# An expert loop with one more block in place of a branch in its middle, and its three compute engines in a written order

## The chip, the cores and the metric

The kernel runs on one core of one Trainium2 chip. The metric is the time of one execution on the device, in microseconds (us). A core has TensorE (PE; its weight loads are shown as PEld), VectorE (DVE), ScalarE (ACT), GpSimd (POOL) and SyncE (SP), each with its own instruction queue; data moves from and to HBM by DMA, which SP, ACT and POOL issue.

## The reference, cut to what matters

A trunk of two layers over 512 tokens of width 1024. Each layer has a mixer, a mixture of experts, and an embedding stage. The change is in the mixture of experts: every token goes to one group of four and in it to the best two of four experts, out of 16.

```python
def hier_moe(x, w_group, b_group, w_router, b_router, w_gate, w_up, w_down):
    ...
    top_v, top_i = lax.top_k(e_sel, TOP_K_IN_GROUP)
    w_k = jax.nn.softmax(top_v, axis=-1) * p_top
    ...
    for e in range(N_EXPERTS):
        he = jax.nn.silu(xt @ w_gate[e]) * (xt @ w_up[e])
        y = y + combine[:, e:e + 1] * (he @ w_down[e])
```

512 tokens with two experts each give 1024 places, 64 for an expert in the mean. A block holds the 128 places of one expert. An expert with more than 128 needs further blocks, which depends on the data; 1024 places fill at most 7 of them.

## The kernel before

All weights stand in one tensor (`wst`) in the order in which they are used: units of 128 x 1024 floats, two of them (1 MB) in a chunk. A block takes 12 units: four for the gate projection, four for the up projection, four for the down projection. `load` (lines 180 to 187) issues one chunk into the next of 14 buffers, which lie in four pools (`RINGS`, line 40); the loads of the loop are issued on SP. `split` (lines 189 to 197) makes from a unit a rounded part `whi` (ACT, line 194) and the remainder `wlo` (DVE, line 195), each with four buffers (`SPLIT`); `mm3` (lines 232 to 235) multiplies with three matmuls, so that the product is nearly that of full floats.

In `moe` (line 925) the router is computed first; it gives the list of places of each expert (`toki`), the list of the further blocks' places (`tokx`, made inside the first block), and `exi` (line 1110), eight integers: for each further block its expert, and in the last the number of further blocks. Then the loop (lines 1238 to 1279) runs over 17 steps: step e gathers the rows of block e+2 (POOL, `gather`), runs gate and up of block e (24 matmuls each), turns the rows of block e+1 (`split_x`: 8 transposes, ACT line 965, DVE line 966), makes the hidden values (`swiglu`, `split_h`: ACT, two DVE operations, 4 transposes, ACT, DVE), and runs the down projection of block e-1 (24 matmuls), whose two halves ACT copies (line 1275) and stores (line 1279, or by halves in line 1277 for the last block). The order on each engine is the scheduler's; the last block's down matmuls run half by half (`DOWN[1]`).

At step `XE` = 5, `further` (line 1187) stands between the hidden values and the down projection: four chunks are loaded ahead, every engine loads the number of further blocks into a register (line 1192), and `blocks` (line 1230) nests seven conditional blocks (`tc.If`, line 1232), each with a whole further block: its weights come by halves of chunks from an address in a register (line 1204), into four single buffers. A conditional block is a unit to the scheduler: nothing from outside moves into it or past it.

After the loop comes `ple` (line 1283), the embedding stage. It loads its first two chunks on SP (lines 1288 and 1289), a third on ACT behind the last store (lines 1291 to 1293), and then runs under a written order for PE, DVE and ACT (`tc.manual_schedule`, line 1295): casts of the first units, 48 matmuls of `project`, the gathers of the expert outputs (line 1312) and so on.

Of the kernel before, what the change touches and what calls it, by code (L numbers as in the profile page):

```python
# [50 lines left out]
XE, XK = 5, 4  # L51

RAWA, RAWB = (2, 3, 1, 0) * 2, (2, 3, 1) * 3
# [53 lines left out]
def tile_hybrid_trunk(ctx, tc, x, wst, gains, small, lam, rwt, cst, out, stop=None):  # L107
# [33 lines left out]
    class W:  # L141
# [8 lines left out]
        base = 0  # L150
# [17 lines left out]
    def pm(shape):  # L168
        return W.psum.tile(shape, F32, name="m", bufs=W.banks["m"])
# [755 lines left out]
    def moe(cx, low, layer):  # L925
# [19 lines left out]
        W.base = FIRST[layer] - PADS[FIRST[layer]]  # L945
# [41 lines left out]
        with ExitStack() as rx:  # L987
# [120 lines left out]
            nc.vector.reduce_sum(exf, xe, axis=AX.X)  # L1108
            nc.vector.tensor_copy(exf[:, 7:8], ext[0:1, 1, NE - 1:NE])
# [57 lines left out]
        with pool_("wk", 2) as wk:  # L1167
# [4 lines left out]
            def swiglu(g, u):  # L1172
                s = wk.tile([128, FF], F32, name="sg", bufs=SB)
                act(s, g, AF.Tanh, scale=0.5)
                stt(s, s, 1.0, g, op0=OP.add, op1=OP.mult)
                tt(s, s, u, op=OP.mult)
                ps = pw([128, 4, 128])
                for f in range(4):
                    nc.tensor.transpose(ps[:, f, :], s[:, f * 128:(f + 1) * 128], ident)  # L1179
                return ps  # L1180

            def split_h(ps, place=None):
                hh, hl = place or [wk.tile([128, 4, 128], F32R, name=n, bufs=HB) for n in ("hh", "hl")]
# [4 lines left out]
            def further(at):  # L1188

                for _ in range(XK):  # L1190
                    ahead()
                nx = nc.values_load(exi[0:1, NX:NX + 1], min_val=0, max_val=NX,
                                    skip_runtime_bounds_check_because="1024 places fill at most 7 further blocks")
                def block(b):
                    ex = nc.sync.value_load(exi[0:1, b:b + 1], min_val=0, max_val=NE - 1)
                    xgx = rows_of(at + 1)
                    nc.gpsimd.indirect_dma_start(out=xgx, out_offset=None, in_=xrow,
                                                 in_offset=bass.IndirectOffsetOnAxis(ap=tokx[:, b:b + 1], axis=0))

                    def part(c, i, a=None):  # L1200
                        n = (RAWA if a else RAWB)[(2 * c + i) % 8]
                        u = wp.tile([128, 1024], F32, name=("wlo", "whi")[n - 2]) if n > 1 else rows_of(at + 1 + n)
                        src = wst[bass.ds(ex * 6 + (FIRST[layer] + c), 1), :, i, :].rearrange("o p b -> (o p) b")
                        nc.sync.dma_start(out=u, in_=src)
                        return split(u, a)

                    split_x(at, xgx)
                    gu = []
                    for m in range(2):
                        ps = pm([128, FF])  # L1210
                        for kp in range(4):
                            w = part(2 * m + kp // 2, kp % 2, 2)
                            for j in range(2):
                                k = 2 * kp + j
                                mm3(ps, xpart(at, k), (w[0][:, j, :], w[1][:, j, :]), k == 0, k == 7)
                        gu.append(ps)
                    hx = rows_of(at + 1, F32R).rearrange("p (h f c) -> p h f c", h=2, f=4)
                    hh, hl = split_h(swiglu(*gu), (hx[:, 0], hx[:, 1]))
                    yp = [pm([128, 512]) for _ in range(2)]
                    for f in range(4):  # L1220
                        w = part(10 + f // 2, f % 2)
                        for nh in range(2):
                            r = slice(nh * 512, (nh + 1) * 512)
                            mm3(yp[nh], (hh[:, f, :], hl[:, f, :]), (w[0][:, r], w[1][:, r]), f == 0, f == 3)
                    y = rows_of(at + 1)
                    for nh in range(2):
                        nc.scalar.copy(y[:, nh * 512:(nh + 1) * 512], yp[nh])
                    nc.scalar.dma_start(out=yrow[(NE + b) * 128:(NE + b + 1) * 128, :], in_=y)

                def blocks(b):  # L1230
                    if b < NX:
                        with tc.If(nx > b):
                            block(b)
                            blocks(b + 1)

                blocks(0)

            hs = None
            for e in range(NE + 1):
                if e < NE:  # L1240
                    if e + 2 < NE:
                        xg.append(gather(toki[:, e + 2:e + 3])[0])
                    gu = []
                    for m in ("gate", "up"):
                        ps = pm([128, FF])
                        for kp in range(4):
                            w = pre.pop(0) if pre else unit(m, 2)
                            for j in range(2):
                                k = 2 * kp + j
                                mm3(ps, xpart(e, k), (w[0][:, j, :], w[1][:, j, :]), k == 0, k == 7)  # L1250
                        gu.append(ps)
                        if m == "gate" and e + 1 < NE:
                            split_x(e + 1, xg[e + 1])
                    if e == 0:

                        wh = wk.tile([128, FF], F32, name="sg", bufs=SB).bitcast(BF)
                        wh = wh.rearrange("p (a t b) -> p a t b", a=2, t=T)
                        nc.vector.tensor_copy(tokx, tokens(slot, wx, NX, wh))
                    with tc.high_priority(offset=40):
                        hh, hl = split_h(swiglu(*gu))  # L1260
                last, hs = hs, (hh, hl)
                if e == XE:
                    further(e)
                if e:
                    yp = [pm([128, 512]) for _ in range(2)]
                    w = {}
                    for f, nh in DOWN[e == NE]:
                        if f not in w:
                            w[f] = unit("down")
                        r = slice(nh * 512, (nh + 1) * 512)  # L1270
                        mm3(yp[nh], (last[0][:, f, :], last[1][:, f, :]), (w[f][0][:, r], w[f][1][:, r]), f == 0, f == 3)
                    y = rows_of(e - 1)
# [254 lines left out]
```

## Time and profile before

| what | value |
|---|---|
| median of three runs | 1467.43 us (1467.11 to 1471.57) |
| the profiled execution's own time | 1475.78 us |
| its span, first to last instruction | 1474.0 us |
| PE busy | 1381.5 us, 94% of the span |
| DVE busy | 1112.3 us, 75% |
| ACT busy | 918.9 us, 62% |
| POOL busy | 127.7 us, 9% |
| mean granted TensorE clock | 0.973 of full speed |

The shares are means over stages that differ. The expert loops run from about 312 to 646 us (layer 0) and from about 1096 to 1400 us (layer 1) of the span. A matmul's duration in the timeline is longer than its step, since matmuls overlap; steps are read from starts. "q" behind an engine's name marks what its sequencer does: issuing DMAs, branches, semaphores, register loads.

### The profile page before, as it was taken

What the parts mean: (1) busy time and instruction counts of PE and PEld (TensorE: products, weight loads), DVE (VectorE), ACT (ScalarE), POOL (GpSimd) and SP (SyncE); (2) the same over time, 40 slices, a digit from 0 to 9 for tenths busy, and PEclk for the clock granted to TensorE, in tenths of its full rate; (3) what the DMA queues carried; (4) which work ended last, traced back from release to release, by engine and by line L of the source; (5) the groups of instructions that cost most, each with busy time, mean ns of one, the idle gap of its engine ahead of it and who ended that gap; (6) DMA issues with size and microseconds to landing.
All of it is one profiled execution on the core that took longest, in us unless ns stands there. A gap on an engine that the chain in (4) does not pass through costs nothing. (4 is left out here: it accounts for less than half of the span.)

```text
span 1474.0 us, 18496 instructions
## 1 busy us (share of the span) xinstructions
PE 1381.5 (94%) x6728; PEld 1091.8 (74%) x6728; DVE 1112.3 (75%) x1573; ACT 918.9 (62%) x1428; POOL 127.7 (9%) x139
## 2 busy tenths in 40 slices
PE   6999999969978999999999999999959979999996
PEld 4766777758856888877878877777648868888775
DVE  5488557689957999977876556665589969999875
ACT  4266654448846888874653545443348858888855
POOL 2010101010000000020020010100010000000030
PEclk9999999979999999999999999999979989999999
DMA  9223124679977999744221111011669979999261
GB/s 343 95 86 129 58 86 172 248 257 381 400 278 290 403 408 408 269 166 192 88 86 57 58 58 57 30 58 61 254 243 346 416 301 390 409 410 386 90 250 58
DMA packets 54650, 323.27 MB, mean 219 GB/s; under 512 B 6480, under 2 KB 6896, under 8 KB 23568
## 3 DMA queue, kind: packets, MB, share of 16 engines
q1 hardware_dynamic: 36576, 250.38, 44.3%
q0 software_dynamic: 12640, 52.16, 9.4%
q10 hardware_dynamic: 5328, 19.40, 3.3%
q8 instruction: 57, 0.93, 0.3%
q14 instruction: 49, 0.40, 0.1%
HBM read 292.55 MB, written 27.26 MB: 217 GB/s over the span
## 5 line engine op out<-in xcount | busy, mean ns | idle before, releaser
L195 DVE TENSOR_TENSOR wlo<-raw,whi 128x1024 fp32r<-128x1024 f32 x478 | 565.0, 1221 | 89.0 <-ACT whi L194 87.0
L194 ACT CAST whi<-raw 128x1024 fp32r<-128x1024 f32 x478 | 492.2, 1055 | 144.4 <-PE m L235 100.7
L233 PE MATMUL m<-whi,eh 128*128 128x512 f32 x528 | 213.9, 405 | 1.6 <-ACT whi L194 1.6
L234 PE MATMUL m<-wlo,eh 128*128 128x512 f32 x528 | 210.9, 399 | 1.6 <-DVE wlo L195 1.5
L235 PE MATMUL m<-whi,el 128*128 128x512 f32 x528 | 210.1, 398 | 0.0
L233 PE MATMUL m<-xth,whi 128*128 128x512 f32 (+1 forms) x368 | 142.9, 389 | 0.6 <-ACT xth L257 0.5
L235 PE MATMUL m<-xth,wlo 128*128 128x512 f32 (+1 forms) x368 | 142.6, 388 | 0.5 <-DVE wlo L195 0.5
L234 PE MATMUL m<-xtl,whi 128*128 128x512 f32 (+1 forms) x368 | 142.0, 386 | 0.8 <-DVE xtl L258 0.8
L234 PEld LDWEIGHTS m<-wlo,eh 128*128 128x128 f32 x528 | 100.5, 190 | 26.6 <-DVE wlo L195 4.2
L233 PE MATMUL m<-whi,xth 128*128 128x512 f32 x288 | 117.0, 406 | 2.7 <-ACT xth L257 1.1
L233 PEld LDWEIGHTS m<-whi,eh 128*128 128x128 f32 x528 | 100.4, 190 | 25.1 <-ACT whi L194 2.1
L235 PEld LDWEIGHTS m<-whi,el 128*128 128x128 f32 x528 | 100.0, 189 | 24.4 <-DVE el L966 0.8
L235 PE MATMUL m<-whi,xtl 128*128 128x512 f32 x288 | 115.7, 403 | 1.6 <-DVE xtl L195 1.0
L234 PE MATMUL m<-wlo,xth 128*128 128x512 f32 x288 | 115.4, 401 | 0.5 <-DVE wlo L195 0.5
L233 PE MATMUL m<-whi,hh 128*128 128x512 f32 x256 | 103.6, 410 | 0.0
L235 PE MATMUL m<-whi,hl 128*128 128x512 f32 x256 | 102.4, 400 | 0.0
L234 PE MATMUL m<-wlo,hh 128*128 128x512 f32 x256 | 102.1, 400 | 0.0
L235 PEld LDWEIGHTS m<-xth,wlo 128*128 128x128 f32 x368 | 70.5, 192 | 12.8 <-DVE wlo L195 1.0
L234 PEld LDWEIGHTS m<-xtl,whi 128*128 128x128 f32 x368 | 70.4, 191 | 12.6 <-DVE xtl L258 1.0
L233 PEld LDWEIGHTS m<-xth,whi 128*128 128x128 f32 x368 | 70.5, 192 | 12.5 <-ACT xth L257 0.9
L973 POOL DMA_INDIRECT xg<-xrow,toki x32 | 34.5, 1079 | 494.8 <-PE w L963 439.2
L965 ACT CAST eh<-w 128x512 fp32r<-128x512 f32 x82 | 46.9, 590 | 39.4 <-PE w L963 38.1
(445 smaller groups left out, 2268.3 us busy)
## 6 DMA issues: line engine op xcount, KB each, us to landing
raw<-in_wst_dram SPq DMA_DIRECT2D x226, 1024.0 KB, 7.5
raw<-in_wst_dram POOLq DMA_DIRECT2D x14, 1024.0 KB, 7.5
yrow<-y ACTq DMA_DIRECT2D x17, 512.0 KB, 8.4
yrow<-gbc ACTq DMA_DIRECT2D x14, 512.0 KB, 8.0
xrow<-raw POOLq DMA_DIRECT2D x8, 512.0 KB, 5.7
yrow<-tmp POOLq DMA_DIRECT2D x14, 256.0 KB, 10.0
h<-in_x_dram SPq DMA_DIRECT2D x4, 512.0 KB, 13.4
whi<-in_wst_dram SPq DMA_DIRECT2D x4, 512.0 KB, 5.4
```

The source lines that it names most:

```text
L194: nc.scalar.copy(hi, src)
L195: nc.vector.tensor_sub(lo, src, hi.bitcast(F32))
L233: mm(ps, l[0], r[0], start=start, stop=False)
L234: mm(ps, l[0], r[1], start=False, stop=False)
L235: mm(ps, l[1], r[0], start=False, stop=stop)
L965: W.turned = nc.scalar.copy(eh[o], ps)
L973: ins = nc.gpsimd.indirect_dma_start(out=xg, out_offset=None, in_=xrow, in_offset=bass.IndirectOffsetOnAxis(ap=idx, axis=0))
```

## The change

The first further block becomes a block of the loop, always run, after expert 5 (`BLOCKS`); where the data needs none, it runs on places that nobody reads (its expert is limited to 15 by a minimum on `exf`). Its six chunks are loaded like the others, from an address in a register of SP. Blocks 2 to 7 stand in nested conditional blocks behind the loop, the outermost with the skipped arm preferred to follow in the code; inside (`rare`) all is single-buffered, and the store is issued by POOL. The register with the number of further blocks is loaded ahead of the loop. From block 1 on the loop stands under a written order for PE, DVE and ACT, in which the casts of a block's units are spread over its own step and the one before.

```diff
-XE, XK = 5, 4
-RAWA, RAWB = (2, 3, 1, 0) * 2, (2, 3, 1) * 3
+BLOCKS = [0, 1, 2, 3, 4, 5, NE] + list(range(6, NE))
+RAWA = (0, 1, 2, 0, 1, 2, 0, 1)
...
-            ring = W.rings[RINGS[(c - W.base - PADS[c]) % len(RINGS)]]
+            ring = W.rings[RINGS[W.count % len(RINGS)]]
+            W.count += 1
...
             nc.vector.reduce_sum(exf, xe, axis=AX.X)
+            ts(exf, exf, NE - 1.0, None, op0=OP.min)
...
-            def further(at):
-                for _ in range(XK):
-                    ahead()
-                nx = nc.values_load(exi[0:1, NX:NX + 1], min_val=0, max_val=NX,
...
-            hs = None
-            for e in range(NE + 1):
...
-                if e == XE:
-                    further(e)
...
+            def rare(at, b):
+                ex = nc.sync.value_load(exi[0:1, b:b + 1], min_val=0, max_val=NE - 1)
...
+                nc.gpsimd.dma_start(out=yrow[(NE + b) * 128:(NE + b + 1) * 128, :], in_=y)
+                if b + 1 < NX:
+                    with tc.If(nx > b + 1, preferred_fallthrough_block=True):
+                        rare(at, b + 1)
+            CHUNK = {"g": 0, "u": 2, "d": 10}
+            extra, parts = {}, {}
+            def chunk(e, m, k):
+                i = CHUNK[m] + k // 2
+                if e == NE:
+                    if i not in extra:
+                        if not extra:
+                            W.ex = nc.sync.value_load(exi[0:1, 0:1], min_val=0, max_val=NE - 1)
+                        src = wst[bass.ds(W.ex * 6 + (FIRST[layer] + i), 1)].rearrange("o p u b -> (o p) u b")
+                        extra[i] = load(src)
+                    return extra[i]
+                c = FIRST[layer] + 6 * e + i
+                if c not in W.loaded:
+                    W.loaded[c] = load(wst[c])
+                return W.loaded[c]
+            def high(e, *units):
+                for m, k in units if e is not None else ():
+                    src = chunk(e, m, k)[:, k % 2, :]
+                    w = [wp.tile([128, 1024], F32R, name=n) for n in ("whi", "wlo")]
+                    nc.scalar.copy(w[0], src)
+                    parts[e, m, k] = src, *w
+            def low_(e, *units):
+                for m, k in units if e is not None else ():
+                    src, hi, lo = parts[e, m, k]
+                    nc.vector.tensor_sub(lo, src, hi.bitcast(F32))
...
+            G, U = [[(m, k) for k in range(4)] for m in "gu"]
+            nx = nc.values_load(exi[0:1, NX:NX + 1], min_val=0, max_val=NX,
...
+            order = ExitStack()
+            order.enter_context(tc.manual_schedule(engines=MS))
+            both(BLOCKS[1], *G, *U[:3])
+            for j, e in list(enumerate(BLOCKS))[1:]:
+                last = BLOCKS[j - 1]
+                q = BLOCKS[j + 1] if j + 1 < len(BLOCKS) else None
+                if j + 2 < len(BLOCKS):
+                    xg.append(rows(BLOCKS[j + 2]))
+                g = pm([128, FF])
+                for k in range(4):
+                    towards(g, j, "g", e, k)
+                turned = [turn_x(j + 1, xg[j + 1], half) for half in range(2)] if q is not None else []
+                s = wk.tile([128, FF], F32, name="sg", bufs=SB)
+                for i in range(3):
+                    if i == 1:
+                        act(s, g, AF.Tanh, scale=0.5)
+                        stt(s, s, 1.0, g, op0=OP.add, op1=OP.mult)
+                    elif turned:
+                        ps, o = turned.pop(0)
+                        nc.scalar.copy(eh[o], ps)
+                        nc.vector.tensor_sub(el[o], ps, eh[o].bitcast(F32))
+                both(e, U[3])
+                both(last, ("d", 0), ("d", 1))
+                u = pm([128, FF])
+                for k in range(4):
+                    towards(u, j, "u", e, k)
+                tt(s, s, u, op=OP.mult)
+                both(last, ("d", 2), ("d", 3))
+                high(q, G[0])
+                yp = [pm([128, 512]) for _ in range(2)]
+                for f in range(2):
+                    down(yp, hs, last, f)
+                now = split_h(turned_s(s))
+                for f in range(2, 4):
+                    down(yp, hs, last, f)
+                low_(q, G[0])
+                both(q, *G[1:3])
+                y = rows_of(j)
+                for nh in range(2):
+                    nc.scalar.copy(y[:, nh * 512:(nh + 1) * 512], yp[nh])
+                store(last, y)
+                hs = now
+                both(q, G[3], *U[:3])
+            e = BLOCKS[-1]
+            both(e, *[("d", f) for f in range(4)])
+            yp = [pm([128, 512]) for _ in range(2)]
+            y = rows_of(len(BLOCKS))
+            for nh in range(2):
+                r = slice(nh * 512, (nh + 1) * 512)
+                for f in range(4):
+                    down(yp, hs, e, f, nh)
+                nc.scalar.copy(y[:, r], yp[nh])
+                put = store(e, y, r)
+            order.close()
+            W.pos = [i for i, u in enumerate(UNITS) if u == ("pp", 0)][layer]
+            W.next = W.pos // 2
+            with tc.If(nx > 1, preferred_fallthrough_block=False):
+                rare(len(BLOCKS) + 1, 1)
```

`both` is `high` (the cast on ACT) followed by `low_` (the remainder on DVE), unit by unit; `towards` gives the six matmuls of one gate or up unit, `down` the matmuls of one down unit, `turn_x` the transposes of the next block's rows, `turned_s` those of the hidden values, `store` the store on ACT.

## Rows read from the trace of the kernel before

**Rows 1.** Busy time by stretch, two stretches of layer 0's expert loop: its undisturbed part, and one period of it. Columns: stretch, its length, busy us (x instructions) of PE, PEld, DVE, ACT and POOL, granted TensorE clock, DMA share, GB/s.
```profile
480.00:640.00 160.00, 160.00 (x742) 130.25 (x741) 151.62 (x150) 134.22 (x158) 5.68 (x6) 1.00 0.85 340
500.00:518.09 18.09, 18.09 (x86) 14.75 (x85) 17.12 (x18) 15.24 (x19) 0.95 (x1) 1.00 1.00 409
```

**Rows 2.** The timeline of PE at the end of layer 0's loop and the start of the next stage. Columns: start us, us, engine, line, operation, output and inputs, tile, count, and in brackets the idle time before it with its releaser. The first row is the first of the last block's down matmuls, the second the last of them (23 steps further); the third is the third matmul of the next stage; the fourth the first transposes of that stage.
```profile
639.99 0.39 PE L233 MATMUL m<-whi,hh 128*128 128x512 f32 x1
645.35 0.39 PE L235 MATMUL m<-whi,hl 128*128 128x512 f32 x1
...
647.02 0.50 PE L235 MATMUL m<-whi,xtl 128*128 128x512 f32 x1 [0.53 <-DVE xtl L195]
...
658.94 1.29 PE L255 MATMUL w<-cs,h 128*128 128x128 f32 x8 [0.92 <-DVE h L1317]
```

**Rows 3.** The timeline of ACT in both loops, the issues of a block's output store alone, on either side of the branch (layer 0: between the second and third row; layer 1: between the sixth and seventh). Columns as in rows 2.
```profile
383.34 0.33 ACTq L1279 DMA_DIRECT2D yrow<-y  x1
401.42 0.33 ACTq L1279 DMA_DIRECT2D yrow<-gbc  x1
...
461.59 0.33 ACTq L1279 DMA_DIRECT2D yrow<-y  x1
478.92 0.33 ACTq L1279 DMA_DIRECT2D yrow<-gbc  x1
...
1167.74 0.33 ACTq L1279 DMA_DIRECT2D yrow<-y  x1
1185.83 0.33 ACTq L1279 DMA_DIRECT2D yrow<-gbc  x1
1215.57 0.34 ACTq L1279 DMA_DIRECT2D yrow<-y  x1
1232.89 0.33 ACTq L1279 DMA_DIRECT2D yrow<-gbc  x1
```

**Rows 4.** The timeline of ACT in the undisturbed period, around the copies of a block's output.
```profile
514.00 1.07 ACT L1275 COPY gbc<-m 128x512 f32<-128x512 f32 x2
514.96 1.07 ACT L194 CAST whi<-raw 128x1024 fp32r<-128x1024 f32 x1
515.10 0.33 ACTq L1279 DMA_DIRECT2D yrow<-gbc  x1
```

**Rows 5.** The timeline of ACT at the end of layer 0's loop. L194 casts one unit of weights, L1275 copies half an output, L1279 and L1277 are stores, L1286 is the next stage's table load.
```profile
638.79 1.05 ACT L194 CAST whi<-raw 128x1024 fp32r<-128x1024 f32 x1 [0.34 <-PE m L235]
639.75 1.07 ACT L1275 COPY y<-m 128x512 f32<-128x512 f32 x2
640.70 1.06 ACT L194 CAST whi<-raw 128x1024 fp32r<-128x1024 f32 x1
643.22 1.05 ACT L194 CAST whi<-raw 128x1024 fp32r<-128x1024 f32 x1 [1.46 <-PE m L235]
...
644.65 1.05 ACT L194 CAST xth<-raw 128x1024 fp32r<-128x1024 f32 x1
...
646.39 0.33 ACTq L1277 DMA_DIRECT2D yrow<-gbc  x1
646.75 1.28 ACT L1286 ACT_TABLE_LOAD   x1 [0.39 <-ACT gbc L1275]
```

**Rows 6.** The timeline of DVE in the undisturbed period: three remainders of weight units in a row.
```profile
512.18 3.48 DVE L195 TENSOR_TENSOR wlo<-raw,whi 128x1024 fp32r<-128x1024 f32 x3
```

**Rows 7.** The branch's own instructions, by engine and operation: those of DVE in layer 1 (two rows), and those of PE's sequencer in layer 0 (three branches, of which the first lets the entered arm follow). Columns: line, engine, operation, count: duration in ns (min/median/max), first and last start in us.
```profile
L1232 DVEq COMPARE_BRANCH  x1: 69/69/69, 1199.7 to 1199.7; - x1
L1232 DVEq EVENT_SEMAPHORE  x1: 21/21/21, 1205.5 to 1205.5; - x1
...
L1232 PEldq COMPARE_BRANCH  x3: 86/192/3848, 414.2 to 451.5; - x3
```

**Rows 8.** Layer 0's branch as SP sees it: SP's semaphore instructions of the branch (columns as in rows 7); the further block's store and its time from issue to landing; SP's first issue of weights after the branch (columns as in rows 2).
```profile
L1232 SPq EVENT_SEMAPHORE  x9: 17/17/17, 444.4 to 452.6; - x9
...
L1228 ACTq DMA_DIRECT2D yrow<-y x1: 331/331/331, 449.7 to 449.7; - x1
...
DMA to landing us min/median/max: 2.9/2.9/2.9
...
452.95 0.35 SPq L186 DMA_DIRECT2D raw<-in_wst_dram  x1
```

**Rows 9.** SP's last issues of weights in layer 0 before the next stage (columns as in rows 7), and three lines of the DMA issues of the whole span: out and in, queue, operation, count, KB each, median us from issue to landing. The third is the store of half the last block's output, the fourth the load that ACT issues behind it.
```profile
L186 SPq DMA_DIRECT2D raw<-in_wst_dram x3: 328/328/328, 602.1 to 607.7; - x3
...
raw<-in_wst_dram SPq DMA_DIRECT2D x226, 1024.0 KB, 7.5
...
yrow<-gbc ACTq DMA_DIRECT2D x4, 256.0 KB, 2.1
...
raw<-in_wst_dram ACTq DMA_DIRECT2D x2, 1024.0 KB, 5.2
```

**Rows 10.** Busy time by stretch behind layer 0's branch; columns as in rows 1.
```profile
452.00:454.00 2.00, 2.00 (x9) 1.97 (x10) 1.46 (x2) 2.00 (x3) 0.00 (x0) 0.50 0.26 41
456.00:458.00 2.00, 2.00 (x8) 1.59 (x8) 1.64 (x3) 1.05 (x1) 0.00 (x0) 0.78 1.04 365
```

**Rows 11.** The register loads of the expert list in both layers, on DVE and on PE's sequencer; columns as in rows 7.
```profile
L1192 PEldq TENSOR_LOAD <-exi x2: 318/402/486, 413.6 to 1198.0; - x2
...
L1192 DVEq TENSOR_LOAD <-exi x2: 316/430/543, 414.9 to 1199.3; - x2
```

More of the change, by code (lines that the diff above doesn't have):

```diff
@@ L1186, in split_h @@
                 return hh, hl
-            def further(at):
-                for _ in range(XK):
-                    ahead()
-                nx = nc.values_load(exi[0:1, NX:NX + 1], min_val=0, max_val=NX,
[L1193 to L1236, printed above, removed]
@@ L1238, in moe @@
-            hs = None
-            for e in range(NE + 1):
[L1240 to L1261, printed above, removed]
-                if e == XE:
-                    further(e)
[L1264 to L1272, printed above, removed]
@@ new lines, in rare, with part @@
+            def rare(at, b):
+                ex = nc.sync.value_load(exi[0:1, b:b + 1], min_val=0, max_val=NE - 1)
+                xgx = rows_of(at)
+                nc.gpsimd.indirect_dma_start(out=xgx, out_offset=None, in_=xrow,
+                                             in_offset=bass.IndirectOffsetOnAxis(ap=tokx[:, b:b + 1], axis=0))
+                def part(c, i, a=None):
+                    n = RAWA[2 * c + i] if a else i
+                    u = wp.tile([128, 1024], F32, name=("wlo", "whi")[n]) if n < 2 else rows_of(at)
+                    src = wst[bass.ds(ex * 6 + (FIRST[layer] + c), 1), :, i, :].rearrange("o p b -> (o p) b")
+                    nc.sync.dma_start(out=u, in_=src)
+                    return split(u, a)
+                split_x(at, xgx)
+                gu = []
+                for m in range(2):
+                    ps = pw([128, FF])
+                    for kp in range(4):
+                        w = part(2 * m + kp // 2, kp % 2, 2)
+                        for j in range(2):
+                            k = 2 * kp + j
+                            mm3(ps, xpart(at, k), (w[0][:, j, :], w[1][:, j, :]), k == 0, k == 7)
+                    gu.append(ps)
+                s = product(*gu, rows_of(at)[:, :FF])
+                hx = rows_of(at, F32R).rearrange("p (h f c) -> p h f c", h=2, f=4)
+                hh, hl = split_h(turned_s(s), (hx[:, 0], hx[:, 1]))
+                yp = [pw([128, 512]) for _ in range(2)]
+                for f in range(4):
+                    w = part(10 + f // 2, f % 2)
@@ new lines, in both, with towards, down @@
+            def both(e, *units):
+                for u in units if e is not None else ():
+                    high(e, u)
+                    low_(e, u)
+            def towards(ps, j, m, e, k):
+                _, *w = parts[e, m, k]
+                w = [a.rearrange("p (a b) -> p a b", a=2) for a in w]
+                for i in range(2):
+                    mm3(ps, xpart(j, 2 * k + i), (w[0][:, i, :], w[1][:, i, :]), k == i == 0, 2 * k + i == 7)
+            def down(yp, h_, e, f, *halves):
+                _, *w = parts[e, "d", f]
+                for nh in halves or range(2):
+                    r = slice(nh * 512, (nh + 1) * 512)
+                    mm3(yp[nh], (h_[0][:, f, :], h_[1][:, f, :]), (w[0][:, r], w[1][:, r]), f == 0, f == 3)
@@ new lines, in turn_x, with store, rows @@
+            def turn_x(j, src, half):
+                ps = pw([128, 4, 128])
+                for d in range(4):
+                    k = 4 * half + d
+                    nc.tensor.transpose(ps[:, d, :], src[:, k * 128:(k + 1) * 128], ident)
+                return ps, (slice(None), j % 2, slice(4 * half, 4 * half + 4))
+            def store(e, y, r=slice(None)):
+                return nc.scalar.dma_start(out=yrow[e * 128:(e + 1) * 128, r], in_=y[:, r])
+            def rows(e):
+                return gather(tokx[:, 0:1] if e == NE else toki[:, e:e + 1])[0]
@@ new lines, in moe @@
+            G, U = [[(m, k) for k in range(4)] for m in "gu"]
+            nx = nc.values_load(exi[0:1, NX:NX + 1], min_val=0, max_val=NX,
+                                skip_runtime_bounds_check_because="1024 places fill at most 7 further blocks")
+            xg.append(rows(BLOCKS[2]))
+            gu = []
+            for m in ("gate", "up"):
+                ps = pm([128, FF])
+                for kp in range(4):
+                    w = pre.pop(0) if pre else unit(m, 2)
+                    for j in range(2):
+                        k = 2 * kp + j
+                        mm3(ps, xpart(0, k), (w[0][:, j, :], w[1][:, j, :]), k == 0, k == 7)
+                gu.append(ps)
+                if m == "gate":
+                    split_x(1, xg[1])
```

31 lines of the change are left out of this document (21 added, 10 removed).

## The prediction

> **What bounds the kernel now.** I read first the busy time by stretch, because the change touches only the expert loop of each layer. In the undisturbed stretch of layer 0's loop PE is busy 160.00 of 160 us, and in one period of it 18.09 of 18.09, with DVE at 17.12 and ACT at 15.24 [rows 1]. The reader should see that TensorE alone sets the pace, that DVE has only 0.97 us to spare in a period, and that a full period costs 18.09 us whatever the queues do. The arithmetic agrees: 72 matmuls in steps of 0.233 us (23 steps from 639.99 to 645.35 [rows 2]) are 16.8, and 12 transposes take what is left.
>
> Next come the issues of the output stores, one for each block, as a clock of the loop [rows 3]. Between branches they stand 18.09 apart. Across layer 0's branch, which runs one further block, the next two distances are 60.17 and 17.33, so 77.50 in place of 36.18: **this branch costs 41.3 us**. Across layer 1's branch, which runs none, they are 29.74 and 17.32: 47.06 in place of 36.18, so **a branch that is not entered costs 10.9 us**. (The 17.3 is the part that is given back, so both are counted over two distances.) One of the two layers needs one further block, the other needs none, and no layer needs a second.
>
> Then the branch's own instructions and the seam behind the loop, since that is where the branch goes.
>
> **The change part by part.** The sum is made against the profiled execution, 1475.8 us (span 1474.0 and 1.8 around it). That is 8.3 above the median of the runs, 1467.43, so differences are added to the median. About 0.3% of it, 4.4 us, is what a measurement can tell from no change.
>
> *The blocks.* Layer 0 loses the 41.3 and gains one period: 18.1 - 41.3 = **-23.2**. Layer 1 loses 10.9 and gains a period that computes nothing of use: 18.1 - 10.9 = **+7.2**. The extra block's six loads, its gather and its store go at the rate of the others (409 GB/s in the period [rows 1], so 7.4 MB) behind PE. Its loads take their address from a register of SP, which costs SP instructions that the 14 loads in flight cover; if the cover is gone it is under a microsecond. [...]
>
> *The fixed order.* In the period the scheduler of before put on ACT three casts, three more, the cast of the hidden values, two casts, two copies and then the next casts. The change writes out the same order, with one difference: the store is issued before the next cast, not behind it. Now the cast starts at 514.96, before the copies end at 515.07, and the store follows at 515.10 [rows 4]. The cast would start at about 515.45, 0.5 us later, and the unit it makes is wanted by PE only 3 us after (18 matmuls into the next block). DVE's 0.97 us of spare time takes it up. I take 0; a gain is excluded because PE is already full, and if the cover fails the price is at most the 0.34 of an issue for each of 32 periods, 11 us.
>
> *The last block.* Here the fixed order matters. Now ACT casts the last block's down weights ahead of and between the copies (638.79, 640.70), so the 24 last matmuls run without a gap, 24 x 0.233 = 5.6 us [rows 2, 5]. In the change all four casts are written behind the two copies and the store of the block before. Count from A, the start of the last down matmuls: copies end at A+0.83, the store is issued until A+1.2, the first cast ends at A+2.25, and four subtractions in steps of 1.16 [rows 6] end at A+7.0. PE can then finish half one (to A+7.4) and run the 12 matmuls of half two (2.8): it ends at A+10.2. That is **+4.6** a layer, 9.2 in all. Waiting behind the copies are DVE's subtractions and through them PE; nothing else fills PE there.
>
> *The branch at the end.* What a branch does is in layer 1's rows [rows 7]: the compare itself takes 0.05 to 0.07 us, but DVE goes on only 5.8 us later (1199.7 to 1205.5), and everything waits for DVE. In the change the skipped arm is the one that follows in the code. In layer 0, where the entered arm follows, PE's shortest compare is 0.09 us. I take 0.1 (nearest row), with 5.8 as the upper end. [...]
>
> What is not free is what stands behind it. [...] Layer 0 shows it: the further block's store was issued at 449.7, landed 2.9 us later, and only then (last of nine, 452.6) did SP pass and issue its next weights at 452.95 [rows 8]. In the change the last store of the loop stands in front of the branch, and the next stage's weights behind it. Now SP issues those some 38 us earlier, at 602.1 to 607.7, against a last store at 646.39 [rows 5, 9]. Let B be the end of the last down matmuls, 645.6 now. The last store is issued at B+0.8, lands 2.1 us later [rows 9], SP issues at B+3.3, 1 MB lands 5.2 us later (the two that ACT issues at this place [rows 9]) at B+8.5. ACT casts two units by B+10.5, DVE has the second remainder at B+11.7, and only then can the third matmul of the next stage run. Now that is at 647.02, B+1.4 [rows 2]. So **+10.3** a layer, 20.6 in all. The ends: 4.3 if SP is not held (then only the table load of 1.28, two casts and a subtraction are in the way, third matmul at B+5.7), 12.6 if the load takes 7.5 like SP's others [rows 9].
>
> *The clock.* After the idle stretch before 451.9 the granted clock was 0.50 and came back at about 456.5 [rows 10]; half of 4.6 us is lost. The same after the new gap: **+2.3** a layer, 4.6 in all. None is lost in the gap of 2.3 us at A, I take it; if it is, 2 more.
>
> *The rest.* The register loads from the expert list move ahead of the loop, 0.3 to 0.54 us each [rows 11], on engines that work there: 0.5 a layer, 1.0. The one added minimum on eight numbers is nothing. Back comes the 0.92 in which PE waits for the gathered rows in the next stage [rows 2], since the stores are late by less (4.6) than PE (14.9): -1.3 over both layers.
>
> Sum: -23.2 + 7.2 + 9.2 + 20.6 + 4.6 + 1.0 - 1.3 = **+18.1**, so 1485.5 us (chance 0.5). Its own range is 1476 to 1496.
>
> **The rivals.** *SP is not held.* If the stores' semaphores are none of those SP brings up, the weights are there and each seam costs 4.3, not 10.3: 18.1 - 12.0 = +6.1, 1473.5. For it: the rare arm's own store has moved from ACT to POOL. Against: its twelve loads a block still use SP's semaphores, and [rows 8] show SP wait for an ACT store. Chance 0.18.
>
> *Faster: the seam is covered.* The blocks save 16.0 us; the edges of the two loops decide, and the point is 8.0 us a layer. If the next stage's weights and casts are as early as now, only the last block's 4.6 and the 0.5 are left: -16.0 + 9.2 + 1.0 = -5.8, 1461.6; with the last casts in time as well, 1452. For it: PE has 24 matmuls in hand while ACT and SP pass the branch. Against: every instruction of the next stage is behind the branch on its engine, and ACT's last copy stands in front. Chance 0.2.
>
> *The fixed order costs in every period.* DVE is at 95%, so the later cast may reach PE: +11 on the forecast, 1496.5. For it: the small slack. Against: the wait is 3 us from its user. A skip that still jumps belongs here too; with SP held its 5.8 lie beside the load. Chance 0.12.
>
> **How the numbers follow.** The likeliest is 1485.5. Faster is most of the second rival, 0.18; within 0.3% is half of the first and a little of the second, 0.12; the rest, 0.70, is slower. The range leaves out the covered seam at its best and the worst of the last rival: 1461 to 1502.
>
> **What would show it.** In the changed profile: stores 18.09 apart through all 17 blocks of both layers, with no gap at the former branch; a gap of PE of 2.3 us before the last down matmuls, and these lasting about 10; SP's next weights issued some 3 us after the last store; PE idle about 10 us there and the clock at 0.50 after it. Wrong would be: weights of the next stage issued long before the last store (first or second rival), or stores more than 18.2 apart (third).

## The result, and the profile after

The kernel with the change takes 1478.79 us (median of 12 runs, 1476.89 to 1483.05), the kernel before beside it on the same chip 1471.64 (12 runs, 1465.41 to 1476.76): ratio **1.0055**, interval 1.0039 to 1.0071, so slower by 8.1 us by this ratio (5.7 to 10.4; the two medians are 7.2 apart). The prediction had the sign and its range held the time, but its sum, +18.1, was more than twice too large. The profiled execution took 1478.86 (span 1476.8).

First the busy time by stretch of the changed kernel: one period of layer 0's loop, as in the second row of [rows 1], and stretches behind the places where PE idles, as in [rows 10].

```profile
500.00:518.09 18.09, 18.09 (x85) 14.74 (x85) 16.96 (x18) 15.03 (x19) 0.95 (x1) 1.00 1.00 398
...
620.00:622.00 2.00, 2.00 (x7) 1.48 (x6) 2.00 (x3) 0.74 (x1) 0.00 (x0) 0.50 0.00 0
...
634.00:636.00 2.00, 2.00 (x7) 1.57 (x6) 0.74 (x1) 1.23 (x2) 1.69 (x3) 0.56 0.86 233
...
1388.00:1392.00 4.00, 4.00 (x11) 3.12 (x10) 2.73 (x3) 0.91 (x1) 0.00 (x0) 0.50 0.01 2
```

The period is untouched: PE fills all of it, DVE has 1.13 us to spare. The stores, read as in [rows 3] from ACT's timeline (some of both layers, the last full period among them), say the same of the whole loop:

```profile
418.41 0.33 ACTq L1297 DMA_DIRECT2D yrow<-gbc  x1
436.50 0.33 ACTq L1297 DMA_DIRECT2D yrow<-y  x1
...
599.27 0.33 ACTq L1297 DMA_DIRECT2D yrow<-gbc  x1
...
1132.32 0.33 ACTq L1297 DMA_DIRECT2D yrow<-y  x1
...
1367.44 0.33 ACTq L1297 DMA_DIRECT2D yrow<-gbc  x1
```

They stand 18.09 apart (599.27 is nine periods behind 436.50, 1367.44 thirteen behind 1132.32); nothing is left of the branches that cost 41.3 and 10.9 us in [rows 3]. What the change costs is at the loop's end. PE's timeline there, to be read beside [rows 2]: the end of the block before, the gaps in the last block's downs, the last down, and the next stage's first matmul and first transposes (L257), in layer 0, then the same of layer 1.

```profile
615.38 0.40 PE L237 MATMUL m<-whi,hl 128*128 128x512 f32 x1
617.95 0.50 PE L235 MATMUL m<-whi,hh 128*128 128x512 f32 x1 [2.17 <-ACT whi L1262]
619.21 0.79 PE L236 MATMUL m<-wlo,hh 128*128 128x512 f32 x1 [0.76 <-DVE wlo L1269]
...
625.75 0.39 PE L237 MATMUL m<-whi,hl 128*128 128x512 f32 x1
630.33 0.80 PE L235 MATMUL m<-whi,xth 128*128 128x512 f32 x1 [4.19 <-ACT xth L196]
...
644.30 1.03 PE L257 MATMUL w<-cs,h 128*128 128x128 f32 x8
...
1386.12 0.50 PE L235 MATMUL m<-whi,hh 128*128 128x512 f32 x1 [2.17 <-ACT whi L1262]
...
1395.40 0.40 PE L237 MATMUL m<-whi,hl 128*128 128x512 f32 x1
1400.70 0.80 PE L235 MATMUL m<-whi,xth 128*128 128x512 f32 x1 [4.90 <-ACT xth L196]
...
1415.43 1.03 PE L257 MATMUL w<-cs,h 128*128 128x128 f32 x8
```

Two places cost time: the last block's downs, which last from 615.6 to 626.0, and the seam behind the branch, where PE idles 4.19 and 4.90 us, not the 10 predicted. ACT's timeline of the same stretch (as [rows 5]; L1364 copies the block before, whose store comes first; L1262 casts the last down weights, L1376 copies the last block's halves, L196 and L1389 are the next stage's casts and table load, L188 a load for it):

```profile
616.43 0.33 ACTq L1297 DMA_DIRECT2D yrow<-y  x1
616.85 3.88 ACT L1262 CAST whi<-raw 128x1024 fp32r<-128x1024 f32 x4 [0.45 <-ACT y L1364]
...
624.00 0.33 ACTq L1297 DMA_DIRECT2D yrow<-gbc  x1
626.18 0.59 ACT L1376 COPY gbc<-m 128x512 f32<-128x512 f32 x1 [2.21 <-PE m L237]
626.66 1.05 ACT L196 CAST whi<-raw 128x1024 fp32r<-128x1024 f32 x1
...
627.19 1.99 ACTq L188 DMA_DIRECT2D raw<-in_wst_dram  x1
627.73 1.28 ACT L1389 ACT_TABLE_LOAD   x1
629.23 1.04 ACT L196 CAST xth<-raw 128x1024 fp32r<-128x1024 f32 x1 [0.22 <-issue]
```

Last the branch of layer 0 (L1381) by engine, with columns as in [rows 7], to be read beside [rows 7, 8]:

```profile
L1381 SPq COMPARE_BRANCH  x2: 38/46/53, 593.3 to 626.4; - x2
...
L1381 PEldq COMPARE_BRANCH  x2: 98/2016/3935, 623.3 to 626.3; - x2
L1381 ACTq COMPARE_BRANCH  x2: 38/44/49, 624.9 to 625.1; - x2
```

And SP's loads for the next stage (L188), in the same columns, where [rows 9] had SP's last issues at 602.1 to 607.7:

```profile
L188 SPq DMA_DIRECT2D raw<-in_wst_dram x2: 327/328/328, 590.3 to 592.6; - x2
```

Three things are to be seen. SP is indeed held at the branch, from 593.3 to 626.4, that is until 2.4 us behind the issue of the store of 624.00 (such a store lands in 2.1 [rows 9]). But the next stage's first two chunks were issued **ahead** of it, at 590.3 and 592.6, and ACT's last copy, and with it the last store, stands **behind** its branch (625.1, then 626.18): here the scheduler moved independent instructions past the conditional block, in both directions. And each engine has two branch instructions: the compare that falls through (98 ns on PE) and then a second one, which I read as a jump over the code that lies in between, the six rare blocks (e9 tests this reading). It takes PE 3.94 us, to 630.3, just when ACT's cast is done too (629.23 and 1.04).

### The profile page after: what moved, and what is told of

Its sections match the earlier page's. It is cut to its first block, busy times and chain, and to the rows that moved or that the text cites. A ratio compares the mean times of both kernels' runs of the same rounds, so it can differ in the third digit from the quotient of the medians.

```text
span 1476.8 us, 18718 instructions
## 1 busy us (share of the span) xinstructions
PE 1392.1 (94%) x6812; PEld 1104.7 (75%) x6812; DVE 1123.4 (76%) x1592; ACT 928.6 (63%) x1446; POOL 132.4 (9%) x140
## 5 line engine op out<-in xcount | busy, mean ns | idle before, releaser
L1269 DVE TENSOR_TENSOR wlo<-raw,whi 128x1024 fp32r<-128x1024 f32 x392 | 456.6, 1219 | 13.8 <-ACT whi L1262 13.7
L1262 ACT CAST whi<-raw 128x1024 fp32r<-128x1024 f32 x392 | 396.0, 1055 | 50.5 <-PE m L237 36.7
L235 PE MATMUL m<-whi,eh 128*128 128x512 f32 x544 | 218.8, 402 | 0.0
L236 PE MATMUL m<-wlo,eh 128*128 128x512 f32 x544 | 215.5, 396 | 0.0
L237 PE MATMUL m<-whi,el 128*128 128x512 f32 x544 | 215.4, 396 | 0.0
L197 DVE TENSOR_TENSOR wlo<-raw,whi 128x1024 fp32r<-128x1024 f32 x110 | 133.3, 1225 | 69.8 <-ACT whi L196 69.5
L196 ACT CAST whi<-raw 128x1024 fp32r<-128x1024 f32 x110 | 113.9, 1050 | 64.6 <-PE m L237 33.3
L235 PE MATMUL m<-whi,hh 128*128 128x512 f32 x272 | 112.1, 412 | 4.3 <-ACT whi L1262 4.3
L236 PE MATMUL m<-wlo,hh 128*128 128x512 f32 x272 | 109.3, 402 | 1.5 <-DVE wlo L1269 1.5
L237 PE MATMUL m<-whi,hl 128*128 128x512 f32 x272 | 108.8, 400 | 0.0
```

Of the source, the lines that this page charges most:

```text
L196: nc.scalar.copy(hi, src)
L197: nc.vector.tensor_sub(lo, src, hi.bitcast(F32))
L235: mm(ps, l[0], r[0], start=start, stop=False)
L236: mm(ps, l[0], r[1], start=False, stop=False)
L237: mm(ps, l[1], r[0], start=False, stop=stop)
L1262: nc.scalar.copy(w[0], src)
```

## The experiments

The theory that the profile of the change suggested (A): two costs of similar size, the last downs behind late casts (some 4 to 5 us a layer) and the seam behind the branch (4 to 5 us), nothing in the loop, and branches of before that cost less at the median than in the one execution that was profiled. The rivals were that one of the two holds all of it, and that a branch's price does not vary. Ratios are to the kernel before on the same chip; 0.001 is 1.47 us. By the ratios' intervals a difference between two kernels below is uncertain by 3 to 5 us.

**e1: no branch behind the loop.** The register loads and further blocks 2 to 7 are left out (this input needs none).

```
-            nx = nc.values_load(exi[0:1, NX:NX + 1], ...)
...
-            with tc.If(nx > 1, preferred_fallthrough_block=False):
-                rare(len(BLOCKS) + 1, 1)
```

> The changed kernel without the conditional block behind the loop and without the register loads for it (this data never enters it). Theory A, the seam is the branch: PE idles 4.2 and 4.9 us behind the last down matmuls because its second branch instruction takes 3.9 and 3.3 us and because the next stage's two casts may not stand ahead of the branch on ACT. Without it the gap falls to about 0.5 and the clock stays up: 4 + 2 us in each layer, 12 less than the changed kernel's 1478.8, so about 1467. Theory B, the gap is ACT's order (copy, cast, table load, cast) and not the branch: it stays near 4, about 1478.

1471.66 us, ratio 1.0008 (0.9988 to 1.0028): 0.0047 or 6.9 us below the change, where 12 were expected. PE's timeline at both seams (last down, next stage's first matmul, its first transposes; layer 0, then layer 1 without the matmul):

```profile
625.93 0.39 PE L237 MATMUL m<-whi,hl 128*128 128x512 f32 x1
626.68 0.50 PE L235 MATMUL m<-whi,xth 128*128 128x512 f32 x1 [0.36 <-ACT xth L196]
...
639.28 1.29 PE L257 MATMUL w<-cs,h 128*128 128x128 f32 x8 [0.17 <-DVE h L1415]
...
1394.31 0.40 PE L237 MATMUL m<-whi,hl 128*128 128x512 f32 x1
...
1407.35 1.16 PE L257 MATMUL w<-cs,h 128*128 128x128 f32 x8
```

The gap is gone, so it is the branch's. At the seams it is worth what the theory said: from the last down to the first transposes PE takes 13.35 and 13.04 us, in the change 18.55 and 20.03, so 5.2 + 7.0 = 12.2 with the clock's part. But layer 0's share did not last in this execution. PE's first transposes in layer 1's loop wait for gathered rows; in the change:

```profile
1079.70 1.94 PE L965 MATMUL w<-cs,xg 128*128 128x128 f32 x8 [5.79 <-DMA xg<-xrow,toki]
```

And in e1:

```profile
1079.48 1.94 PE L965 MATMUL w<-cs,xg 128*128 128x128 f32 x8 [10.14 <-DMA xg<-xrow,toki]
```

They start at the same time in both. In all other profiles here this wait is 5.6 to 6.6 us; whether other executions of e1 wait so long, and for what, is open.

**e2: the last block's casts first.** The last down weights are cast where another block would cast its next one's gate weights, ahead of and around the copies. Nothing is left out.

```
-                high(q, G[0])
+                z, D = (q, G) if q is not None else (e, [("d", f) for f in range(4)])
+                high(z, D[0])
...
-            both(e, *[("d", f) for f in range(4)])
```

> The changed kernel with the last block's four down casts and remainders in the places that a next block's first four gate units would have, ahead of and right behind the two copies. Theory A, these 4.6 us a layer (and the clock that falls in their gap, 1 to 2 us) are lost to the written order: the last down matmuls run in 5.6 us and not in 10.4 and 11.9, about 10 to 13 less than 1478.8, so 1466 to 1469, with the gap behind the branch unchanged at 4 to 5. Theory B, the time is only moved: PE ends earlier but waits longer behind the branch, 1476 to 1479.

1470.85 us, ratio 1.0000 (0.9984 to 1.0017): 0.0055 or 8.1 us below the change, 4.0 a layer. Two stores of layer 0 (ACT's timeline), of the block before and of the last block's first half, show where:

```profile
616.28 0.33 ACTq L1297 DMA_DIRECT2D yrow<-y  x1
620.38 0.33 ACTq L1297 DMA_DIRECT2D yrow<-gbc  x1
```

The first half's store comes 4.10 behind the block before, not 7.57 (616.43 to 624.00).

**e3: both.** e1 and e2 in one kernel, further blocks 2 to 7 left out.

> Both edits together, no branch and the last casts first. Theory A: the two losses are apart and add, so the blocks' own saving of 16 us against the kernel before stands alone: about 1471.6 - 15 = 1457. Theory B, one loss hides the other: no better than the better of the two, 1466.

1462.72 us, ratio 0.9942 (0.9925 to 0.9960): 16.6 us below the change, where 6.9 and 8.1 make 15.0. The two costs add up; neither hides the other, and without both the change would be faster than before by 0.6%. At the seams e3 takes 13.37 and 13.03 us from the last down to the first transposes, e2 18.35 and 19.42: 11.4 less, of which the time keeps 8.5. So here too part of the gain is lost later: at layer 0's seam e3 gains 5.0 us on e2, of which 1.8 is left when layer 1's first gathered rows come.

**e4: the next stage's weights issued late.** This puts in what the prediction had assumed, that the two chunks are issued behind the last store (here by ACT, in the prediction by SP).

```
-        for i in range(2):
-            ahead(pool=PLACE(i))
+        with tc.issue_after(put.ins):
+            for i in range(2):
+                ahead(nc.scalar, PLACE(i))
```

> The changed kernel with the next stage's first two chunks issued by ACT behind the last store, as the prediction had them, and not some 33 us earlier by SP. Theory A (the prediction's price was right for weights that come late): 1 MB lands 5 to 7 us after its issue at about B+1.6, two casts and a remainder follow, the third matmul of the next stage runs at about B+11 and not at B+5.7: 5 us in each layer and some clock, 1489 to 1492. Theory B, what bounds the seam is PE's branch and ACT's table load, and the loads lie beside them: under 3 us in each layer, 1479 to 1484.

1489.68 us (6 runs), ratio 1.0126 (1.0098 to 1.0154), 10.4 us above the change. PE's timeline, layer 0 and layer 1:

```profile
636.76 0.79 PE L235 MATMUL m<-whi,xth 128*128 128x512 f32 x1 [9.25 <-ACT xth L196]
...
1412.40 0.79 PE L235 MATMUL m<-whi,xth 128*128 128x512 f32 x1 [10.47 <-ACT xth L196]
```

What ACT's cast waits for, from its timeline in layer 0:

```profile
634.72 1.04 ACT L196 CAST whi<-raw 128x1024 fp32r<-128x1024 f32 x1 [4.90 <-DMA raw<-in_wst_dram]
```

The third matmul of the next stage comes 10.7 and 11.9 us behind the last down (638.21 and 1413.85), where the prediction had 11.7. Its price for late weights was right; in the change they are not late.

**e5: the kernel before without its branches.** Layer 0's further block, a part of the result, is left out.

```
-                if e == XE:
-                    further(e)
```

> The kernel before without its branch, its further blocks and their register loads (layer 0's further block is left out). It measures what the change removes. By the store distances of the profiled execution the two branches cost 41.3 + 10.9 = 52.2 us: 1471.7 - 52.2 = 1419.5. Rival: the profiled execution of the kernel before is some 4 us above its median because its branches take longer under the profiler than otherwise (all of its executions spread over 12 us, those of the kernels without a branch over 8); then the saving is 46 to 49, 1423 to 1426.

1419.67 us (5 runs), ratio 0.9679 (0.9658 to 0.9701): the two branches together cost 47.1 us (43.9 to 50.3), not the 52.2 of the profiled execution. (The time is theory A's 1419.5 only because the kernel before took 1467.13 beside it, not 1471.7.)

**e6: the change without its extra blocks.** Layer 0's further block is left out.

```
-BLOCKS = [0, 1, 2, 3, 4, 5, NE] + list(range(6, NE))
+BLOCKS = list(range(NE))
```

> The changed kernel without the extra block (layer 0's further block is left out), the written order and the branch behind the loop kept. It measures what the extra block costs. Theory A: one period in each layer, 2 x 18.09 = 36.2 less than 1478.8, 1442.6. Against e5, which has neither block nor branch, what is left over is the price of the order and of the two seams: 17 to 23 us by the sum's terms as the changed trace shows them. Rival: the extra block also costs DMA time or a wait, 38 or more.

1440.79 us (5 runs), ratio 0.9819 (0.9799 to 0.9838): 0.0236 or 34.7 us below the change, so an extra block costs 17.4, within the error of its 18.09. Against e5, the same blocks with the old loop end, it is slower by 0.0140, **20.6 us: all that the two loop ends cost**, since in both the stores inside the loop stand 18.09 apart.

**e7: the order left to the scheduler.** The hand-written order of the loop is taken out.

```
-            order.enter_context(tc.manual_schedule(engines=MS))
...
-            order.close()
```

> The changed kernel with the loop's written order taken away, so that the scheduler sets the order of PE, DVE and ACT; blocks and branch as in the change. Theory A: the written order gains nothing in the loop (18.09 us from store to store in both) and loses about 4.5 us a layer at the last block, so 8 to 10 less, 1469 to 1471. Theory B: it is needed because the scheduler, given the code in this form, feeds PE worse: over 1479.

1472.06 us, ratio 1.0021 (1.0004 to 1.0038): 5 us below the change. The stores stay 18.09 apart, so the order is worth nothing inside the loop, and costs at its end, where the scheduler casts the last weights earlier. PE's gaps at the seams stay, 6.40 and 4.53.

**e8: the kernel before, once more**, to see whether a branch's price varies.

> The kernel before once more with a profile. Theory A, the first profiled execution was typical: span within 2 us of 1474, 41.3 and 10.9 us at the two branches. Theory B, the branches vary from execution to execution: these two differ by 2 us or more from the first profile.

1468.57 us (one execution). ACT's stores around layer 1's branch, as in [rows 3]:

```profile
1182.36 0.33 ACTq L1279 DMA_DIRECT2D yrow<-gbc  x1
...
1208.71 0.34 ACTq L1279 DMA_DIRECT2D yrow<-y  x1
1226.02 0.33 ACTq L1279 DMA_DIRECT2D yrow<-gbc  x1
```

And what ended PE's idle time in it, from PE's timeline, with DVE's instructions of this branch (columns as in [rows 7]):

```profile
1199.29 1.94 PE L963 MATMUL w<-cs,xg 128*128 128x128 f32 x8 [4.13 <-DVEq L1232]
...
L1232 DVEq COMPARE_BRANCH  x1: 69/69/69, 1196.2 to 1196.2; - x1
...
L1232 DVEq EVENT_SEMAPHORE  x1: 21/21/21, 1199.2 to 1199.2; - x1
```

The same matmul in the first profile of the kernel before:

```profile
1205.59 1.94 PE L963 MATMUL w<-cs,xg 128*128 128x128 f32 x8 [6.95 <-DVEq L1232]
```

The two distances are 26.35 and 17.31, so this branch cost 7.5 us, not 10.9. The price varies from one execution to the next, with the same code and the same data (the first profile's chip is not on record; on one chip the executions of this kernel spread over 13 us). What varied is on DVE: from its compare to its next instruction it took 3.0 us here and 5.8 in [rows 7]. Layer 0's distances are 59.27 and 17.30 here, so its branch cost 40.4. Together that is 47.9, near e5's 47.1, in an execution near the median. So being profiled does not by itself make the branches dear, as e5's rival had it.

**e9 to e11: what the gap at the seam is made of.** All three build on e2, where PE idles 3.98 and 5.31 us. e9 cuts the code behind the branch to one rare block (3 to 7 are left out), so that PE's jump is short (the first edit below); e10 moves the next stage's table load behind the cast of its input (the second); e11 does both.

```
-                if b + 1 < NX:
+                if b + 1 < 2:
...
-        tc.keep_in_program_order(nc.scalar.preload_act_table_set("natural_log_exp_and_others"))
...
         pe_ = unit("p", None, ...)
+        tc.keep_in_program_order(nc.scalar.preload_act_table_set("natural_log_exp_and_others"))
```

> This is the last block with its casts first, with the code behind the branch cut to one rare block (its rare blocks 3 to 7 are left out), so that TensorE's jump over it is short. In the kernel with casts first TensorE's own jump ends at 626.1 us and ScalarE's cast of the next stage's input at 626.4, in the second layer at 1390.5 and 1392.3: two chains that end nearly together. Theory A (both chains are needed): TensorE's second branch falls from 3.4 and 3.3 us to under 0.5, but its gap stays at 3.6 to 4.0 us in the first layer and 4.5 to 5.3 in the second, since ScalarE's chain (copy, cast, store, issue, table load, cast) is as long; the time stays at that of casts first, about 1471 us, within 2 us. Rival B (the far jump alone holds the engines, ScalarE's too): the gap falls to 1 to 2 us in both layers and the time by 5 to 7 us, to 1464 to 1466 us.

> This is the last block with its casts first, with the next stage's table load moved behind ScalarE's cast of that stage's input (nothing left out). ScalarE's chain behind the branch gets shorter by the table load's 1.28 us. Theory A (two chains end together): in the first layer the gap falls by no more than 0.3 us, since TensorE's jump ends at 626.1 us; in the second, where ScalarE ends 1.8 us behind the jump, it falls by about 1.3 us; the time falls by 1 to 2 us, to about 1469.5 us. Rival B (only ScalarE's chain counts): the gap falls by 1.3 us in both layers and the time by 2.6 us or a little more. Rival C (the far jump alone counts): nothing changes.

> Both edits together: short code behind the branch (rare blocks 3 to 7 left out) and the table load behind the cast. Theory A (two chains end together): now both are shorter, so the gap falls by about 1.3 us in both layers, to some 2.7 and 4.0 us, and the time by 2.6 to 4 us against casts first, to about 1467.5 us. Rival B (only ScalarE's chain counts): the same as with the table load moved alone. Rival C (the far jump alone counts): the same as with the short code alone.

e9: 1469.18 us, ratio 0.9981 (0.9961 to 1.0000). e10: 1471.52, 1.0003 (0.9987 to 1.0020). e11: 1468.85, 0.9975 (0.9958 to 0.9993). The times differ from e2's 1.0000 by less than their intervals; the gaps tell more. For each kernel first PE's branches in layer 0 (columns as in [rows 7]), then PE's next matmul from its timeline, in e10 with ACT's cast that it waits for between the two. In e9:

```profile
L1382 PEldq COMPARE_BRANCH  x2: 98/139/180, 619.2 to 622.3; - x2
...
626.08 0.80 PE L235 MATMUL m<-whi,xth 128*128 128x512 f32 x1 [3.98 <-ACT xth L196]
```

In e10:

```profile
L1382 PEldq COMPARE_BRANCH  x2: 98/1925/3752, 621.5 to 624.5; - x2
...
627.26 1.04 ACT L196 CAST xth<-raw 128x1024 fp32r<-128x1024 f32 x1 [1.34 <-issue]
...
628.36 0.65 PE L235 MATMUL m<-whi,xth 128*128 128x512 f32 x1 [4.01 <-ACT xth L196]
```

In e11 (its jump takes 0.18 as in e9):

```profile
625.98 0.50 PE L235 MATMUL m<-whi,xth 128*128 128x512 f32 x1 [2.63 <-ACT xth L196]
```

In layer 0 the short jump alone (0.18 in place of 3.4) leaves the gap as it was, since ACT's copy, cast, table load and cast take as long; with the table load out of the way as well it is 2.63. e10 does not test the far jump alone there: its cast did not come earlier, because ACT's issue of one load took 1.84 us (0.44 in e9) where the table load had been. The cast ended at 628.30, PE's jump at 628.25. In layer 1 of e10 the cast did come earlier (1.56 us behind the copy, in e2 2.84), the gap fell from 5.31 to 4.07, and the jump and the cast ended together at 1393.4. So two chains end nearly together, PE's jump and ACT's work, as theory A had it.

In layer 1 there is more, which theory A did not have: e9's gap fell from 5.31 to 3.98. ACT's last copy there (its timeline), in e2:

```profile
1388.43 0.59 ACT L1377 COPY gbc<-m 128x512 f32<-128x512 f32 x1 [3.55 <-issue]
```

And in e9:

```profile
1385.91 0.59 ACT L1377 COPY gbc<-m 128x512 f32<-128x512 f32 x1 [2.21 <-PE m L237]
```

In e9 the copy follows PE's last down (1385.47 and 0.39) at once. In e2 it starts 1.4 us after that down has ended (1386.66 and 0.39), 2.6 us behind ACT's second branch at 1385.8. So with the far jump ACT is held too (the record of its own branch is 0.04 us long), and rival B of e9 was right in its mechanism there, though not in its size. (With the far jump e10's copy is 1.4 us late too, with the short one e11's is not.) e11's gap stayed at 4.29 in layer 1, since ACT's issue of one load took 2.13 us there ahead of the cast. What sets the length of that issue is open. Each of these gaps is read from one execution.

No kernel here that keeps all further blocks was faster than before: e2 and e10 tie with it.

## Why the prediction was right and wrong

**Right.** The period: stores 18.09 apart through all blocks, no cost of the fixed order, no cost of the extra block beyond its 18.09 (398 GB/s in the period and PE never waiting). The last block: predicted gap 2.3 and downs of 10.2 us, measured 2.17 + 0.76 and 10.4 in layer 0 (615.6 to 626.0); e2 gives 4.0 a layer for the 4.6. The clock does fall to 0.50 behind that gap (620 to 622), where the prediction took no loss, with 2 more if there were one: in layer 1, where 1388 to 1392 has 0.50, the downs took until 1395.6, 1.7 more than forecast. The 0.92 of waiting for gathered rows came back: PE's first transposes of that stage wait for nothing. The fall-through compare took 0.1 (98 ns on PE in layer 0, 81 in layer 1).

**Wrong: the step "what is not free is what stands behind it", 10.3 us a layer.** It said that the next stage's weights are issued behind the branch, since nothing moves into or past a conditional block. That premise, also in the description of the kernel above, is false: the two chunks went out ahead of the branch at 590.3 and 592.6. That SP is held there was right (593.3 to 626.4 in layer 0, to the last of its nine semaphore instructions; what each of them waits for no run shows) and cost nothing, since SP's next load comes only after 642. In the step's place the seam took 5.2 and 7.0 us more than without the branch (e1) up to the next stage's first transposes, clock included, where the prediction had 10.3 and 2.3 a layer; of these 12.2 the whole time shows 6.9. They come from chains that end together: a second branch on PE that jumps over the rare code (3.94 and 3.32 us), and ACT's last copy, two casts and table load, in layer 1 with ACT's own jump ahead of them. The prediction gave the fall-through 0.1, with 5.8 as the upper end; it missed that the way to the join is a jump of its own. PE's second branch took 3.94 us over six rare blocks and, in e9, 0.18 over one (both layer 0): in these runs the skip was short only where the join was near. Why the far one takes so long no run shows.

**Wrong in size: the branch that goes.** 41.3 and 10.9 were read from one execution that lay 8.3 above its median. At the median both together cost 47.1 (e5), and another execution has 7.5 for the second (e8). So the blocks give 36.2 - 47.1 = -10.9, not -16.0.

**The sum as measured**, in us over both layers: -10.9 for the blocks; 8.1 for the last downs (e2) and 6.9 for the seam (e1), 16.6 for both (e3); some 4 left at the loop's end (20.6 less 16.6). Of these e3's last downs hold 2.8: from the first start to the last they take 6.75 us in either layer (614.88 to 621.63 in layer 0), in the kernel before 5.36 [rows 2], with PE waiting for DVE's remainders. The rest was not located. Total -10.9 + 20.6 = +9.7, against 8.1 (5.7 to 10.4) measured; with the 34.7 that e6 gives for the blocks in place of 36.2 the sum closes of itself, being made of differences of the same kernels, so it is no test. The register loads (0.29 to 0.55 us on ACT, PE and DVE) were placed right in front of the branch, not ahead of the loop, and are part of e1's 6.9.

**What was luck.** The outcome lies nearest the first rival's +6.1, whose condition (the weights are not late) came true by another way than it named: SP was held, but had no more to issue. And the sign came out right because of the error: the seam, its clock and the register loads were put at 26.2 and measured 6.9, and with that in place of them and every other term as predicted the sum is -1.2. The branches that go were too dear as well, by 5.1, which pulls the other way.

## What to carry to other kernels

A branch moved out of the loop was not free there (5.2 and 7.0 us at the two seams; the whole time shows 6.9 of them): look at the join, what each engine must jump over, and what the next stage has already in flight when it comes. Before you price what waits behind a branch, find where the scheduler put it; in e4 it took a dependence to keep the loads there. And where the work of a loop's end was interleaved by the scheduler, a fixed order for the steady period has to be written out for the last round as well: that alone cost as much as the branch (8.1 us, e2, against 6.9, e1). Follow a gain to the end of the program before you count it: in e1 a wait further on took part of it back (10.14 us for gathered rows, 5.79 in the change).

## What the runs showed of the hardware

Where a conditional block fell through, it took its compare (0.03 to 0.1 us) and then a second branch, whose time on PE went with the code in between: 3.3 to 3.9 us over six rare blocks (the change, e2, e10), 0.18 in layer 0 and 0.31 in layer 1 over one (e9, e11). On ACT and DVE a branch's own record is short (0.03 to 0.07 us), and the time goes by before the next instruction: ACT's came 2.6 us behind the branch of layer 1 in the first profile of the kernel before (1199.0 to 1201.6), and as late in layer 1 of e2 (1385.8 to 1388.43); DVE's came 5.8 us behind it in that profile of the kernel before and 3.0 in the other (e8). What holds them in that time no profile names.

In layer 0 of the change the granted clock was 0.50 in 620 to 622, after gaps of 2.17 and 0.76 us, and behind the longer gap from 626.1 to 630.3 it was still 0.56 in 634 to 636. A single DMA issue on ACT's queue took between 0.44 us (e9, layer 0) and 2.13 us (e11, layer 1) at the same place in the program.
